# PEER's two tiles of tokens taken one after the other, the first one's listed products in plain float32 beside the second one's routing

## The chip, the cores and the metric

The kernel runs on one core of a Trainium2 chip. The metric is device time in microseconds (us), the median of three runs; lower is better. Engines are named as in the profile: PE multiplies matrices (PEld is its weight load), DVE and ACT work on vectors, POOL issues the indirect transfers, SP issues the ordinary ones.

## The reference, cut to what matters

Two transformer blocks run over 256 tokens of width 1024. Only the last part of the second block is touched by the change, the PEER layer, which picks experts by product keys:

```python
def retrieve(xb):                       # a block of 128 tokens, 8 heads
    q = (xb @ wq).reshape(128, 8, 2, 128)
    s = jnp.einsum('tphq,phkq->tphk', q, keys)            # 2 x 128 scores a head
    top_s, top_i = lax.top_k(s, 16)
    cand = top_s[:, :, 0, :, None] + top_s[:, :, 1, None, :]
    best_s, best_c = lax.top_k(cand.reshape(128, 8, 256), 16)
    i1 = jnp.take_along_axis(top_i[:, :, 0], best_c // 16, axis=-1)
    i2 = jnp.take_along_axis(top_i[:, :, 1], best_c % 16, axis=-1)
    idx = i1 * 128 + i2                                   # one of 16384 experts
    g = jax.nn.softmax(best_s, axis=-1)
    act = gelu(jnp.einsum('tpkd,td->tpk', u_tab[idx], xb))
    return jnp.einsum('tpk,tpkd->td', g * act, v_tab[idx])
```

Every token thus uses 128 (8 x 16) of 16384 experts, each with a row of 1024 numbers in `u_tab` and another in `v_tab`. After it come a residual sum and a last norm.

## The kernel before, in words

The first block and the mixer of the second end at about 702 us of the traced execution; `peer()` is the rest. It never works token by token. It sees the experts as 128 rows (partitions) by 128 columns j, and needs the table A[row, j, token] of weights, which is nonzero for the chosen experts alone. Its steps, for the 256 tokens at once, in two tiles of 128:

- **Heads.** `head(h)` makes the queries of a head for both tiles (16 float32 matmuls 128x256, L1695, each shown in the trace as two passes) and the key scores (4 matmuls, L1708). `topk` (L1490 to L1518) then runs on DVE for both tiles. One `chunk()` per head stands between: 16 float32 matmuls of the same line that make the u products of two columns of all experts ("dense" columns). 19 chunks give D = 38 dense columns in all.
- **Weights and groups.** `weights()` makes softmax weights and transposes the indices. Then 64 groups of 4 tokens: DVE compares an iota with the indices (`o`, L1752) and weights the result (`ow`, L1753), ACT makes `od` (L1754), PE multiplies them (12 float16 matmuls, L1767 and L1769; the latter sums the gates over tokens, the mask of used experts), and the result goes into A (DVE L1773 multiplies it into the dense columns, ACT L1774 copies the rest).
- **Listing.** For the other 90 columns, `listing` packs the experts that occur at all into short lists, in blocks of 4 column pairs (DVE `oq` L1586, ACT `dq` L1588, PE L1597), and writes their row numbers, `rowV` and `rowA`. A goes to tables in DRAM (`keep`).
- **Listed pairs.** A pair is two listed columns of 128 experts. POOL fetches their u and v rows (`uv`, L1879) and their rows of A (`araw`, L1883) by indirect DMA. PE transposes u (L1895), ACT and DVE split it and v into two fp32r parts (L1866, L1867), PE makes u products (`first`, 24 fp32r matmuls 128x256 per tile: three products for one in float32), and then the v products (`second`, 12 fp32r matmuls 128x512 per tile) into the sums `po`. There are 23 pairs with u and v and 10 with v alone (for dense columns). Some serve one tile and some both, 29 and 14 tile passes in all. `uv` has 6 buffers, three pairs' worth.
- **The end.** A branch that handles experts beyond the lists, the residual sum, and the norm.

Each engine works through its own queue in order. A scheduler fixes that order when the program is built: it moves instructions past each other within the queue as far as dependencies and its own time model allow, so program text and queue may differ widely.

## Time and profile before

| | us |
|---|---|
| median of three runs | 1282.18 (1279.02 to 1282.44) |
| the profiled execution's own time | 1270.43 |
| its span in the trace | 1268.4 |
| PE, DVE, ACT, POOL busy in it | 1177.4, 998.0, 664.2, 171.0 |

The span is measured from the first to the last instruction; the profiled execution's own time is 2.03 us longer, and it is 11.75 us below the median of the runs shown. All positions below are us from the start of the span. The busy shares are averages over very different stages, so what follows goes by stage.

### The profile page before, as it was taken

Reading aid. Unit: us, or ns where it says so; the run is one execution under the profiler, and the core shown is the slowest. Engines: PE = TensorE matmul, PEld = TensorE weight load, DVE = VectorE, ACT = ScalarE, POOL = GpSimd, SP = SyncE. Lnnn points to the kernel's source line nnn. Section 1 sums busy time; section 2 is a strip of 40 time slices with the busy share of each in tenths; the row PEclk is TensorE's granted clock in tenths of the full one; section 3 lists DMA queues with packets and bytes.
Section 4 is the critical chain, followed back from the end, with each engine's and each line's share of the span. In section 5 each row is a group of like instructions: output and inputs, shape, how many; then the busy total and the mean of one; then the engine's idle time right before and its main releaser. Section 6 shows DMA issues by size and latency. Waiting matters only on the chain. (4 is left out here: it accounts for less than half of the span.)

```text
span 1268.4 us, 20024 instructions
## 1 busy us (share of the span) xinstructions
PE 1177.4 (93%) x7329; PEld 1024.2 (81%) x7329; DVE 998.0 (79%) x2245; ACT 664.2 (52%) x1118; POOL 171.0 (13%) x169
## 2 busy tenths in 40 slices
PE   8999889999999989999999999989883799999986
PEld 7877667789999878897988888879883688888875
DVE  8999988669988877777887599978887677545766
ACT  6665566644644455657644211146656666444653
POOL 3000000000000000000100000000000756444750
PEclk9999899999999999998999999989996799999998
DMA  6651147647899955554335445422849988556761
GB/s 239 209 170 46 35 157 257 225 133 249 264 307 320 311 194 178 170 161 122 117 92 174 136 150 157 142 91 84 226 141 281 394 326 316 202 175 227 272 224 66
DMA packets 92519, 245.42 MB, mean 193 GB/s; under 512 B 7712, under 2 KB 43200, under 8 KB 85888
## 3 DMA queue, kind: packets, MB, share of 16 engines
q1 hardware_dynamic: 79744, 176.72, 43.8%
q0 software_dynamic: 12672, 67.38, 14.6%
q8 instruction: 59, 0.97, 0.3%
q14 instruction: 44, 0.36, 0.1%
HBM read 224.91 MB, written 19.15 MB: 192 GB/s over the span
## 5 line engine op out<-in xcount | busy, mean ns | idle before, releaser
L209 ACT ACTIVATE whi<-raw 128x1024 fp32r<-128x1024 f32 x176 | 185.4, 1058 | 173.0 <-PE g L216 48.4
L210 DVE TENSOR_TENSOR wlo<-raw,whi 128x1024 fp32r<-128x1024 f32 x176 | 214.7, 1223 | 52.6 <-ACT whi L209 51.6
L1695 PE MATMUL g<-hf,raw 128*128 128x256 f32 x864 | 195.3, 384 | 3.1 <-DVE A L1788 1.6
L1695 PEld LDWEIGHTS g<-hf,raw 128*128 128x128 f32 x864 | 163.2, 192 | 24.7 <-ACT A L1790 2.0
L214 PE MATMUL g<-hfh,whi 128*128 128x256 f32 x352 | 100.7, 287 | 2.6 <-DVE ft L879 2.5
L216 PE MATMUL g<-hfh,wlo 128*128 128x256 f32 x352 | 99.0, 286 | 1.6 <-DVE wlo L210 1.6
L215 PE MATMUL g<-hfl,whi 128*128 128x256 f32 x352 | 100.0, 285 | 0.0
L1879 POOL DMA_INDIRECT uv<-in_uv,rowV x46 | 55.0, 1195 | 323.0 <-DVE rowA L1613 281.3
L1867 DVE TENSOR_TENSOR ul<-ut,uh 128x512 fp32r<-128x512 f32 x92 | 61.9, 687 | 36.8 <-ACT uh L1866 36.4
L1867 DVE TENSOR_TENSOR vl<-uv,vh 128x1024 fp32r<-128x1024 f32 x46 | 56.3, 1226 | 27.2 <-ACT vh L1866 25.2
L1866 ACT ACTIVATE uh<-ut 128x512 fp32r<-128x512 f32 x92 | 52.9, 593 | 45.9 <-PE ut L1895 45.0
L214 PE MATMUL g<-vh,ah 128*128 128x512 f32 x168 | 67.9, 408 | 7.1 <-PEq L1993 3.6
L214 PEld LDWEIGHTS g<-hfh,whi 128*128 128x128 f32 x352 | 67.1, 191 | 3.9 <-DVE ft L879 2.7
L215 PE MATMUL us<-ul,h2h 128*128 128x256 f32 x232 | 68.5, 295 | 0.9 <-DVE ul L1867 0.9
L214 PE MATMUL us<-uh,h2h 128*128 128x256 f32 x232 | 68.7, 296 | 0.2 <-ACT uh L1866 0.2
L216 PEld LDWEIGHTS g<-hfh,wlo 128*128 128x128 f32 x352 | 66.4, 190 | 2.3 <-DVE wlo L210 2.2
L215 PEld LDWEIGHTS g<-hfl,whi 128*128 128x128 f32 x352 | 67.0, 190 | 0.0
L215 PE MATMUL g<-vl,ah 128*128 128x512 f32 x168 | 66.5, 398 | 0.0
L216 PE MATMUL us<-uh,h2l 128*128 128x256 f32 x232 | 65.9, 284 | 0.0
L924 DVE SCALAR_TENSOR_TENSOR wmod<-wmod,cc 128x1024 f32<-128x1024 f32 x48 | 58.7, 1223 | 7.9 <-DMA wmod<-in_w_mod 6.7
L1866 ACT ACTIVATE vh<-uv 128x1024 fp32r<-128x1024 f32 x46 | 48.6, 1058 | 30.0 <-PE g L216 27.6
L216 PE MATMUL g<-vh,al 128*128 128x512 f32 x168 | 63.7, 404 | 0.0
(661 smaller groups left out, 3140.2 us busy)
## 6 DMA issues: line engine op xcount, KB each, us to landing
wmod<-in_w_mod SPq DMA_DIRECT2D x48, 512.0 KB, 5.8
raw<-in_ffn_in SPq DMA_DIRECT2D x44, 512.0 KB, 5.4
raw<-in_pu SPq DMA_DIRECT2D x38, 512.0 KB, 3.7
raw<-in_ffn_out SPq DMA_DIRECT2D x22, 512.0 KB, 4.6
Gd<-A SPq DMA_DIRECT2D x22, 512.0 KB, 6.7
raw<-in_w_out SPq DMA_DIRECT2D x16, 512.0 KB, 3.8
raw<-in_pwq SPq DMA_DIRECT2D x16, 512.0 KB, 3.8
raw<-in_w_qkv SPq DMA_DIRECT2D x12, 512.0 KB, 4.4
```

Source lines behind the costliest of these rows:

```text
L209: self.S.activation(hi, raw, AF.Copy)
L210: self.last_lo = self.V.tensor_sub(lo, raw, hi.bitcast(F32))
L214: a = self.T.matmul(out, ahi, bhi, start=start, stop=False, skip_group_check=True)
L215: self.T.matmul(out, ahi, blo, start=False, stop=False, skip_group_check=True)
L216: b = self.T.matmul(out, alo, bhi, start=False, stop=stop, skip_group_check=True)
L924: i = V.scalar_tensor_tensor(o, w, 1.0, cc[:, j], op0=OP.mult, op1=OP.mult, accum_out=acc)
L1695: T.matmul(p[:, g], w[g][:, k * 128:(k + 1) * 128], hf[:, k], start=k + g == 0, stop=k == 7, skip_group_check=True)
L1866: S.activation(hi, z, AF.Copy)
L1867: V.tensor_sub(lo, z, hi.bitcast(F32))
L1879: P.indirect_dma_start(raw[j], None, vs if k else uv, bass.IndirectOffsetOnAxis(rowV[:, n:n + 1], 0))
```

## The change

Everything in PEER that was done for both tiles together is now done for each tile (`route(tt)`, `listing(..., tt, ...)`, tables and lists per tile), and the two are to overlap: tile 0 is routed and listed first, then its listed pairs run, and `route(1)`, a generator, is stepped between them against a budget of 9 us per pair (8.2 for a top-k of one head, 3.0 for the weights, 1.5 for a group, 1.6 for a listing block). `head(h)` still makes the scores of both tiles; tile 1's are kept in `later` (`sc_7022` in the queues). Dense columns fall from 38 to 14 (7 chunks), so 114 columns are listed, per tile, in 18 u+v pairs and 3 v-only pairs (`caps`), 42 pairs in all. Tile 0's pairs are not split: ACT copies the transposed u, `one` is 8 float32 matmuls 128x256 (L1878) and `two` is 4 float32 matmuls 128x512 (L1908), which read the fetched v itself. Tile 1's pairs keep the three fp32r products. The buffers of `ow` and `od` fall from 3 to 2, those of the dense weights from 5 to 4.

```diff
-        D = 38
-        lims = ((16, 28, 46), (6, 12, 20))
-        NS = 128 - D
+        D = 14
+        caps = (36, 6)
+        NK = (128 - D, D)
...
-            tabs = [dram("Gd", [128 * NS + 128, 256]), dram("Ad", [128 * D + 128, 256])]
+            tabs = [[dram(n + str(tt), [128 * m + 128, 128]) for n, m in zip("GA", NK)] for tt in range(2)]
...
-            rp = rs.enter_context(self.pool("w2", 5))
+            ws0 = ExitStack()
+            rp = ws0.enter_context(self.pool("w2", 4))
...
+            A = [None, None]
+            rt = ExitStack()
+            A[1] = rt.enter_context(self.pool("pa1", side="right")).tile([128, 128, 128], F32, name="A1")
+            qp = rt.enter_context(self.pool("pq", side="right"))
+            op = rt.enter_context(self.pool("oh", AHEAD, side="right"))
+            A[0] = ws0.enter_context(self.pool("pa0")).tile([128, 128, 128], F32, name="A0")
+            later = qp.tile([128, 8, 2, 128], F32, name="sc1")
...
-                s = qp.tile([128, 2, 2, 128], F32, name="sc", bufs=2)
-                S.activation(s, p, AF.Copy)
+                s = qp.tile([128, 2, 128], F32, name="sc", bufs=2)
+                S.activation(s, p[:, 0], AF.Copy)
+                S.activation(later[:, h], p[:, 1], AF.Copy)
...
-            def group(t0, j0):
-                while len(ready) < AHEAD and spread.t < 256:
-                    spread(spread.t)
-                    spread.t += NT
+            def group(t0, tt, j0):
...
+            def keep(tt, want):
                 for k, (lo, hi) in enumerate(((D, 128), (0, min(D, 2 * now["chunk"])))):
...
-            sc = head(0)
...
-            for h in range(8):
-                self.topk(sc, h, qp, idx, best)
+                    while want and now["tokens"][tt] == 128 and kept[k, tt] < hi - lo:
+                        a = kept[k, tt]
+                        b = kept[k, tt] = min(hi - lo, a + 8)
+                        m = NK[k]
+                        i = self.D.dma_start(tabs[tt][k][0:128 * m].rearrange("(p j) t -> p j t", j=m)[:, a:b],
+                                             A[tt][:, lo + a:lo + b])
+                        self.order(self.last_load, i)
+                        want -= 1
...
+            def route(tt, sc):
+                idx = qp.tile([128, 2, 128], F32, name="idx")
+                best = qp.tile([128, 128], F32, name="best")
+                it, wt = (qp.tile([128, 64, 2, 2], F16, name=n) for n in ("idxT", "wgtT"))
+                for h in range(8):
+                    self.topk(sc(h), h, qp, idx, best)
+                    yield 8.2
+                weights(idx, best, it, wt)
+                yield 3.0
+                t0 = 0
+                for g in range(128 // NT):
+                    while len(ready) < AHEAD and t0 < 128:
+                        spread(t0, it, wt)
+                        t0 += NT
+                    group(g * NT, tt, 2 * now["chunk"])
+                    now["tokens"][tt] += NT
+                    yield 1.5
...
+            scs = [head(0)]
+            def first_tile(h):
                 if h < 7:
-                    sc = head(h + 1)
-                chunk()
-            weights()
-            qs.close()
-            with self.pool("oh", AHEAD + 1) as op[0]:
-                for g in range(256 // NT):
-                    if g % 10 == 4:
-                        chunk()
-                    group(g * NT, 2 * now["chunk"])
-                    now["tokens"] += NT
-                    if g % 3 == 2:
-                        keep()
...
-            lister = self.listing(gates, has, f32(it)[:, 0:128], pc, D, lims)
-            rowA, rowV, left = next(lister)
+                    scs.append(head(h + 1))
+                return scs[h]
+            for n, _ in enumerate(route(0, first_tile)):
+                if n in (12, 22, 32):
+                    chunk()
...
+            lister = self.listing(mask, L, has[:, 0], place[:, 0], pc, 0, D, caps)
+            got[0] = next(lister)
             while now["chunk"] < D // 2:
                 chunk()
-                keep(3)
+                keep(0, 4)
                 for _ in range(4):
                     next(lister, None)
-            keep(99)
+            keep(0, 99)
             for _ in lister:
                 pass
...
+            ws0.close()
...
+                    def fetch(s):
+                        o = caps[0] if s.k else 0
+                        ra, rv, _ = got[s.tt]
+                        s.at = vp.tile([128, 2, 128], F32, name="araw", bufs=3)
+                        s.raw = [vp.tile([128, 1024], F32, name="vraw", bufs=2) if s.k else
+                                 vp.tile([128, 2048], F32, name="uv", bufs=6) for _ in range(2)]
+                        for j in range(2):
+                            n = o + 2 * s.c + j
+                            P.indirect_dma_start(s.raw[j], None, vs if s.k else uv,
+                                                 bass.IndirectOffsetOnAxis(rv[:, n:n + 1], 0))
+                        for j in range(2):
+                            n = o + 2 * s.c + j
+                            P.indirect_dma_start(s.at[:, j], None, tabs[s.tt][s.k],
+                                                 bass.IndirectOffsetOnAxis(ra[:, n:n + 1], 0))
+                    def turn(s):
+                        if s.k:
+                            return
+                        s.u = [xp[0].tile([128, 8, 256], F32R, name="u" + n) for n in "hl"] if s.exact else \
+                            [vp.tile([128, 8, 256], F32, name="u")]
+                        for a in range(4):
+                            p = pg.tile([128, 2, 256], F32, name="g").rearrange("p b (j e) -> p b j e", j=2)
+                            for b in range(2):
+                                for j in range(2):
+                                    n = (2 * a + b) * 128
+                                    T.transpose(p[:, b, j], s.raw[j][:, n:n + 128], self.ident)
...
+                            if s.exact:
+                                split(p, *(z[:, n] for z in s.u))
+                            else:
+                                S.activation(s.u[0][:, n], p, AF.Copy)
+                            yield
...
+                        p = self.pst.tile([128, 256], F32, name="t")
+                        for k in range(8):
+                            if s.exact:
+                                self.mm3(p, act.hi[:, k, s.t], act.lo[:, k, s.t], s.u[0][:, k], s.u[1][:, k],
+                                         k == 0, k == 7)
+                            else:
+                                T.matmul(p, hf[:, k, s.t], s.u[0][:, k], start=k == 0, stop=k == 7)
...
+                        v = [z if s.k else z[:, 1024:2048] for z in s.raw]
+                        if s.exact:
+                            s.a = split(a, *(xp[0].tile([128, 2, 128], F32R, name="a" + n) for n in "hl"))
+                            s.v = [split(z, *(xp[0].tile([128, 1024], F32R, name="v" + n, bufs=3) for n in "hl"))
+                                   for z in v]
+                        else:
+                            s.a, s.v = (a,), [(z,) for z in v]
...
+                            if s.exact:
+                                m = self.mm3(po[s.tt][b], *a, *w, start, stop)
+                            else:
+                                m = [T.matmul(po[s.tt][b], a[0], w[0], start=start, stop=stop,
+                                              skip_group_check=True)] * 2
...
+                n0, n1 = caps[0] // 2, caps[1] // 2
+                cols = [(0, c) for c in range(n0)]
+                for c in range(n1):
+                    cols.insert(3 + c * 4, (1, c))
+                NC = len(cols)
+                pairs = [Pair(tt, k, c, tt == 1, n == 0, n == NC - 1) for tt in range(2)
+                         for n, (k, c) in enumerate(cols)]
+                more = route(1, lambda h: later[:, h])
+                budget, fetched, back = 0.0, 0, None
+                act = None
+                NP = len(pairs)
+                for i in range(-1, NP + 1):
+                    if i == NC - 2:
+                        for _ in more:
+                            pass
+                        for _ in lister:
+                            pass
+                        keep(1, 99)
+                        rt.close()
+                        rps.close()
+                        xp.append(ws.enter_context(self.pool("px", 2, side="right")))
+                        for k in range(8):
+                            split(hf[:, k], act.hi[:, k], act.lo[:, k])
+                        x = xp[0].tile([128, 2, 1024], F32, name="x", bufs=1)
+                    while fetched < min(NP if i >= NC - 2 else NC, i + 3):
+                        pairs[fetched].fetch()
+                        fetched += 1
+                    turn = iter(pairs[i + 1].turn() or ()) if i + 1 < NP else iter(())
+                    cur = pairs[i] if 0 <= i < NP else None
+                    if cur:
+                        cur.one()
+                    for _ in range(2):
+                        next(turn, None)
+                    if cur:
+                        cur.weigh()
+                    for _ in turn:
+                        pass
+                    if i < NC - 2:
+                        budget += 9.0
+                        while budget > 0 and more:
+                            t = next(more, None)
+                            if t is None:
+                                more = ()
+                                lister = self.listing(mask, L, has[:, 1], place[:, 1], pc, 1, D, caps)
+                                got[1] = next(lister)
+                                t = 6.0
+                            budget -= t
+                        if not more:
+                            keep(1, 6)
+                            while budget > 0:
+                                next(lister, None)
+                                budget -= 1.6
+                    if i == NP - 3:
+                        left = self.sm.tile([128, 1], F32, name="left")
+                        n = self.nc.values_load(ln[0:1, 0:1], min_val=0, max_val=32768,
+                        with self.tc.If(n > 0):
+                            rest()
+                        self.D.dma_start(x.rearrange("p t d -> p (t d)"), xd)
+                        norm(0)
+                    if back:
+                        back.two()
+                    back = cur
+                norm(1)
```

`topk`, `weights`, `chunk` and `listing` are cut to one tile in the same manner, with half the elements in each instruction that handled both.

What this makes of the queues can be read from the built programs. First DVE, in the groups of tile 0 (A is the table, `t` the product of a group in PSUM). Before:

```order
L1753 TENSOR_TENSOR ow<-o,wgtT 128x1024
L1752 TENSOR_TENSOR o<-iof,idxT 128x1024
L1773 TENSOR_TENSOR A<-A,t 128x16x4
L1753 TENSOR_TENSOR ow<-o,wgtT 128x1024
L1773 TENSOR_TENSOR A<-A,t 128x16x4
```

And now, at the same place (`A_7021` is tile 0's table, `tks`, `tky`, `tkz`, `tki`, `tkf` are top-k's tiles, and `sc_7022` holds the scores of tile 1):

```order
L1489 MATCH_REPLACE tky<-tks,sc_7022 128x128
L1758 TENSOR_TENSOR A_7021<-A_7021,g 128x2x56
L1724 TENSOR_TENSOR o<-iof,idxT 128x1024
L1725 TENSOR_TENSOR ow<-o,wgtT 128x1024
L1513 TENSOR_TENSOR tkz<-tkz,tkf 128x512
L1490 MAX tks<-tky 128x8
L1743 TENSOR_TENSOR A_7021<-A_7021,t 128x4x4 x2
L1725 TENSOR_TENSOR ow<-o,wgtT 128x1024
L1724 TENSOR_TENSOR o<-iof,idxT 128x1024
L1514 TENSOR_REDUCE idx<-tkz 128x2x16
L1493 CAST tkf<-tki 128x32
```

Tile 1's top-k, which the program text puts beside tile 0's pairs, stands in DVE's queue between tile 0's groups. Counted along the queue, the heads of tile 1 end after groups 6, 10, 18, 20, 28 and 30 of tile 0's 32, and the last two within the first two listing blocks of tile 0; none is left beside tile 0's pairs.

Next PE, in a pair of tile 0 after all routing (`g<-ident,uv` are transposes of u, `t<-u,hf` is `one`, `t<-ident,us` the transposes in `weigh`, `po<-uv,ua` is `two`):

```order
L1908 MATMUL po<-uv,ua 128x512 x4
L1878 MATMUL t<-u,hf 128x256 x2
L1859 MATMUL g<-ident,uv 128x128 x8
L1888 MATMUL t<-ident,us 128x128 x2
L1878 MATMUL t<-u,hf 128x256 x2
L1859 MATMUL g<-ident,uv 128x128 x4
L1878 MATMUL t<-u,hf 128x256 x4
L1859 MATMUL g<-ident,uv 128x128 x4
```

The four `po` matmuls are the last readers of a pair's `uv` buffers, and the same buffers are transposed from again three pairs on. The transposes of the next pair start one `t<-u,hf` block after each `po` block.

Last PE again, where tile 1's indices are transposed (L1705) beside the first pairs of tile 0, after seven of them, and its groups begin (`od`, `ow`):

```order
L1888 MATMUL t<-ident,us 128x128 x2
L1705 MATMUL t<-ident,idx 128x128 x2
L1705 MATMUL t<-ident,best 128x128
L1859 MATMUL g<-ident,uv 128x128 x4
L1908 MATMUL po<-uv,ua 128x512 x4
L1908 MATMUL po<-vraw,araw 128x512 x4
L1859 MATMUL g<-ident,uv 128x128 x5
L1736 LDWEIGHTS od
```

In the queue there follow nine groups of tile 1 with nothing but 23 transposes among them, then a pair for every six groups or so, and the last six groups again without a product of a pair.

## Rows read from the trace of the kernel before

**Rows 1.** The page's part 1, PE.

```profile
PE 1177.4 (93%) x7329; PEld 1024.2 (81%) x7329; DVE 998.0 (79%) x2245; ACT 664.2 (52%) x1118; POOL 171.0 (13%) x169
```

**Rows 2.** Busy us by stretch: PE, PEld, DVE, ACT, POOL; PEclk, DMA, GB/s.

```profile
714.70:831.10 116.40, 110.89 (x541) 98.13 (x539) 114.37 (x495) 17.30 (x27) 0.00 (x0) 0.99 0.50 150
836.00:941.50 105.50, 100.61 (x984) 91.20 (x983) 87.76 (x190) 66.55 (x135) 0.00 (x0) 1.00 0.49 142
941.50:956.70 15.20, 11.25 (x90) 9.76 (x89) 10.27 (x29) 3.92 (x8) 0.00 (x0) 1.00 0.72 198
956.70:990.30 33.60, 10.98 (x130) 9.68 (x131) 22.84 (x71) 26.20 (x36) 7.23 (x8) 0.54 1.01 294
1000.00:1220.00 220.00, 216.37 (x1397) 192.67 (x1397) 138.14 (x191) 120.82 (x191) 127.67 (x114) 1.00 0.74 266
```

**Rows 3.** PE in order of time, heads: start us, us, instruction.

```profile
719.02 1.05 PE L1708 MATMUL t<-keys,pq 128*128 128x128 f32 x8
719.92 11.82 PE L1695 MATMUL g<-hf,raw 128*128 128x256 f32 x54
731.57 1.06 PE L1708 MATMUL t<-keys,pq 128*128 128x128 f32 x8
```

**Rows 4.** The waits in the groups, 836 to 941.5: total, times, longest.

```profile
DVE A L1773 <- PE t L1767: 15.6, 13, 3.4
```

**Rows 5.** Groups of instructions by line, PEER alone: busy us, mean ns.

```profile
L1752 DVE TENSOR_TENSOR o<-iof,idxT 128x1024 f16<-128x1024 f16 x64 | 43.6, 689 | 2.1 <-ACT od L1754 0.8
L1753 DVE TENSOR_TENSOR ow<-o,wgtT 128x1024 f16<-128x1024 f16 x64 | 43.6, 688 | 0.0
L1773 DVE TENSOR_TENSOR A<-A,t 128x72 f32<-128x72 f32 (+6 forms) x64 | 15.0, 246 | 16.6 <-PE t L1767 16.6
```

**Rows 6.** DVE in order of time, the first comparison of the groups.

```profile
833.06 1.28 DVE L1752 TENSOR_TENSOR o<-iof,idxT 128x1024 f16<-128x1024 f16 x2
```

**Rows 7.** PE in order of time, float16 matmuls of the groups.

```profile
912.16 0.62 PE L1767 MATMUL t<-ow,od 128*128 128x128 f16 x8
912.62 0.39 PE L1769 MATMUL gates<-ow,od 128*128 128x128 f16 x4
```

**Rows 8.** DVE in order of time, two listing blocks.

```profile
956.75 0.69 DVE L1586 TENSOR_TENSOR oq<-iof,pq 128x1024 f16<-128x1024 f16 x1
958.62 0.69 DVE L1586 TENSOR_TENSOR oq<-iof,pq 128x1024 f16<-128x1024 f16 x1 [0.54 <-ACT dq L1588]
```

**Rows 9.** All engines in order of time, from list to first pair.

```profile
980.94 1.12 POOL L1879 DMA_INDIRECT uv<-in_uv,rowV  x1 [281.29 <-DVE rowA L1613]
983.79 0.95 POOL L1883 DMA_INDIRECT araw<-Gd,rowA  x1 [0.31 <-issue]
983.86 0.69 DVE L1586 TENSOR_TENSOR oq<-iof,pq 128x1024 f16<-128x1024 f16 x1 [0.68 <-ACT dq L1588]
990.30 1.08 PE L1895 MATMUL ut<-ident,uv 128*128 128x128 f32 x3
```

**Rows 10.** PE in order of time, the listed pairs.

```profile
1061.42 0.39 PE L216 MATMUL g<-vh,al 128*128 128x512 f32 x1
1061.64 0.28 PE L215 MATMUL us<-ul,h2h 128*128 128x256 f32 x1
1061.76 0.28 PE L216 MATMUL us<-uh,h2l 128*128 128x256 f32 x1
1062.24 1.04 PE L1895 MATMUL ut<-ident,uv 128*128 128x128 f32 x8
1063.03 0.48 PE L214 MATMUL g<-vh,ah 128*128 128x512 f32 x1
```

**Rows 11.** Indirect transfers of 990 to 1230: issues, median us to landing.

```profile
uv<-in_uv,rowV POOLq DMA_INDIRECT x42, 7.7
```

**Rows 12.** PE's wait at the branch; then the chain's first step after PE.

```profile
1235.59 0.77 PE L214 MATMUL g<-vh,ah 128*128 128x512 f32 x1 [3.60 <-PEq L1993]
1258.02 0.70 DVE gy L2008
```

More of the change, by code (lines that the diff above doesn't have):

```diff
@@ L1521, in listing @@
-    def listing(self, gates, has, place, pc, D, lims):
+        tf, c2 = (tp.tile([128, 2, 16], F16, name=n) for n in ("tkf", "tkc2"))
+        z = tp.tile([128, 256], F32, name="tkz")
+        t = tp.tile([128, 2, 16], F32, name="tks")
+        ti = tp.tile([128, 2, 16], U32, name="tki")
+        for p in range(2):
+            x = sc[:, p]
+            y = tp.tile([128, 128], F32, name="tky")
+            V.max(t[:, p, 0:8], x)
+            V.match_replace(y, t[:, p, 0:8], x, -3e38)
+            V.max(t[:, p, 8:16], y)
+            V.max_index(ti[:, p, 0:8], t[:, p, 0:8], x)
+            V.max_index(ti[:, p, 8:16], t[:, p, 8:16], y)
@@ L1576, in listing @@
-            cp = ls.enter_context(self.pool("blk", side="right"))
+            new, before, rk = (cp.tile([128, 128], F32, name=n) for n in ("new", "before", "rk"))
+            P.memset(new, 1.0)
+            P.memset(new[:, 0:1], 0.0)
+            P.memset(new[:, D:D + 1], 0.0)
+            V.tensor_scalar(before, self.jp, 0.0, None, op0=OP.is_gt)
+            V.tensor_scalar(has, mask, 0.0, None, op0=OP.is_gt)
+            V.tensor_tensor_scan(rk, new, has, 0.0, op0=OP.mult, op1=OP.add)
+            p = self.pst.tile([128, 2], F32, name="t")
@@ new lines, in listing @@
+            for n, r in enumerate(keys):
+                T.matmul(p[:, n:n + 1], before, rk[:, r.stop - 1:r.stop], start=n == 0, stop=True,
+                         skip_group_check=True)
+            base = self.sm.tile([128, 2], F32, name="base")
+            V.tensor_copy(base, p)
+            for n, r in enumerate(keys):
+                V.scalar_tensor_tensor(place[:, r], rk[:, r], base[:, n:n + 1], has[:, r], op0=OP.add, op1=OP.mult)
+            V.tensor_scalar(place, place, -1.0, None, op0=OP.add)
@@ L1847, in peer @@
[L1847 to L1857 removed]
+            halves = slice(0, 512), slice(512, 1024)
@@ new lines, in two @@
+                            a, w = [z[:, j] for z in s.a], [z[:, halves[b]] for z in s.v[j]]
+                            start, stop = s.first and j == 0, s.last and j == 1
+                            if s.exact:
[3 more added lines that the diff above has]
+                                              skip_group_check=True)] * 2
```

450 lines of the change are left out of this document (152 added, 298 removed).

## Prediction

> **What bounds the kernel now.** I read the busy shares first, then the same by stretch of PEER, then the waits, and only then single instructions. PE is busy 93% of the span [rows 1], but PEER's stretches have different bounds [rows 2]. While the heads are scored (714.7 to 831.1) DVE is busy for 114.4 of 116.4 us: 16 top-k passes (8 heads, two tiles) at 7.15 us each, with PE's dense chunks beside them. In the groups (836 to 941.5) PE is busy for 100.6 of 105.5, DVE for 87.8, and DVE's largest wait is 15.6 us for a group's product [rows 4]. From 941.5 to 990.3 PE is busy for only 22.2 of 48.8 us: lists are made, and the first pair is awaited. In 1000 to 1220, the listed pairs, PE is busy for 216.4 of 220. So there are 27 us of idle PE between groups and pairs to win, and 10.4 after PE's last product, from 1258.0 to the end at 1268.4 [rows 12].
>
> **PE's prices.** After a keys block, 54 float32 passes 128x256 run from 719.92 to 731.57 [rows 3]: 0.216 us each, 0.43 for a matmul of two, 6.9 for 16. A keys block takes 0.90. In the pairs an fp32r matmul 128x256 starts 0.12 after the one before, one of 128x512 takes 0.22 to 0.23, and 8 transposes 0.79, 0.099 each [rows 10]. A group's 12 float16 matmuls take 0.69, since 8 take 0.46 [rows 7].
>
> A check of them on the old loop: 23 pairs x 16 transposes (36), 29 x 24 first products (84), 29 x 0.25 for weighing (7) and 504 second products (116) make 243 us. The loop took 1258.0 - 990.3 = 267.7 [rows 9, 12], of which some 8.5 at the branch (PE's wait there is 3.6 [rows 12]; by my estimate the reload of x holds as much again, and the rest is slower clock), so about 16 us, 7%, were lost otherwise.
>
> **The change: PE's work.** 12 fewer chunks save 12 x 6.9 = 83 us. A u+v pair of tile 0 costs 16 x 0.099 + 8 x 0.43 + 0.25 + 4 float32 matmuls 128x512. No float32 matmul of that width stands in these rows. As low bound I take three fp32r products (0.69), as high bound two passes each as long as a whole fp32r row (2 x 0.48 = 0.96 [rows 10]); I use 0.86, twice the 256-wide one, which is the same two passes. That is 8.7 us; a v-only pair is 3.4. 18 and 3 of them make 167. A pair of tile 1 costs 1.58 + 24 x 0.12 + 0.25 + 12 x 0.23 = 7.5, a v-only one 2.8: 143 in all. Together 310 against 243 before, 67 more. So on PE alone the change saves 83 - 67 = 16 us; with the 27 above, 43 is the most it can win, if nothing new stands idle. The rest of the forecast is what stands idle.
>
> **Heads.** Top-k now runs for one tile while the heads are scored, so PE sets the pace: 16 x 0.43 + 0.90 = 7.8 per head. Seven heads after the first score at 714.7 end at 769.3, and the last top-k 7.15 later, at 776.5 instead of 831.1: 54.6 gained. The first comparison followed 2 us behind that [rows 6], so it now starts at 778.5.
>
> **Tile 0's groups.** Here the order decides. Tile 1's eight top-k passes stand in DVE's queue within these groups and just behind, about 6.45 of them before the last group. DVE has 32 x 1.38 (`o` and `ow` [rows 5]) = 44, 32 small multiplications at about 0.1 = 3 (0.25 before, on up to 38 columns, now 2 to 6), 6.45 x 7.15 = 46 of top-k, and 1 for chunks and weights: 94 us. PE has 32 x 0.69 and 48 dense matmuls in that time, 43 us, so DVE sets the end: 778.5 + 94 = 873, against 941.5. Without tile 1's top-k it would be 827. That work is not new, but it was to lie beside tile 0's pairs, where DVE has little else to do, and now it stands ahead of everything that waits for tile 0's list.
>
> **Tile 0's list.** A block takes 958.62 - 956.75 = 1.87 [rows 8], the single `oq` buffer going from DVE to ACT and back; 15 blocks instead of 12 stand before the first fetch: 28. The prologue took 15.2 [rows 2]; with one class instead of three and no chunk in it I take 9 (bounds 5 and 15). 1.55 top-k heads are left, 11 us, of which gaps between blocks take perhaps 6: 5 more. So the first fetch goes out at 873 + 42 = 915, and the first transposes follow 9.4 later, as before (980.94 to 990.30 [rows 9]): 925. That is 65 us earlier than before.
>
> **Tile 0's pairs.** 167 of pairs, 22 for tile 1's 32 groups on PE, 10 for its list (PE's 11.0 in 956.7 to 990.3 bounds it [rows 2]) and 1 of transposes: 200 at PE's pace. On top:
> - 8 for the start: the granted clock was 0.54 in the stretch ahead of the pairs, close to the 1.2 GHz level, where PE was busy for 11 of 33.6 us [rows 2]; it will be so again, and I take it that 8 us of the first work cost twice their time.
> - 10 for fetches. A pair's `uv` buffers are free only after its `two`, and are transposed from three pairs later; by the queue, 8.7 + 0.86 = 9.6 us of PE work lie between. A fetch takes 1.1 to issue and 7.7 to land [rows 9, 11], the second column 1.3 more: 10.1. So about 0.5 us late in each of 18 pairs. Before, v was split into copies, which freed the buffer earlier.
> - 17 for tile 1's groups. The first nine and the last six have no products of pairs among them, and go at DVE's pace, 1.55 against 0.69: 13. The `ow` buffers are two now, so bursts of four groups wait too: 4.
> - 8 for tile 1's listing, 17 blocks of which some wait at 1.87 with little else in the queue; 4 for the 8.4 MB of tile 1's table, written beside the fetches (29 us of full DMA at 294 GB/s [rows 2], mostly in idle share); 2 at the boundary of the tiles.
> These 49 (24% of 200) are the softest part: 7% as in the old loop would be 14, and fetches 3 us late would be 45 more.
>
> Taking away tile 0's splits saves nothing: in 1000 to 1220 DVE and ACT were busy for 138 and 121 of 220 [rows 2], so PE covered them.
>
> **Tile 1's pairs and the end.** 143, plus 5 for fetches and 8 for branch and reload of x: 156. Then 10.4.
>
> **Sum.** 925 + 200 + 49 + 156 + 10.4 = 1340.4 against a span of 1268.4: 72 longer. The profiled execution of before took 1270.4 and the median is 1282.2; adding 72 to the median gives **1354**.
>
> **A rule against the trace.** Fetch issues by POOL now run beside DVE's comparisons for half of the pairs. One row shows it: an `araw` issue at 983.79 took 0.95 while a comparison ran from 983.86 for 0.69 [rows 9], no longer than issues elsewhere. The Trainium skill, "SBUF — State Buffer", section "Who interferes with whom", says that GpSimd and some VectorE instructions (two-port modes, or two SBUF inputs against a GpSimd read) exclude each other on a shared port pair, one blocking until the other has finished. By that rule issues would be held in those pairs; by the row they are not. I go by the row, and price the other as a rival.
>
> **Rivals.**
> 1. *Tile 1's top-k hides in waits of tile 0's groups.* For it: DVE did wait 15.6 us in 64 groups. Against it: that is 8 in 32, and there are 46 to hide, in a stretch where PE has only 43 us of work. If it hid wholly, everything comes 46 earlier: 1308. Chance 7%.
> 2. *Faster.* The mechanism is overlap at PE's own pace: PE never waits for tile 1's routing or for fetches, so the loops lose 7% as before (24 instead of the 54 above, 30 less). By itself that gives 1324, within my forecast's own range. To end faster it needs the list of tile 0 early too: it decides at first transposes before about 883 (925 - 42), which means the groups done by 831, where I have 873. With rival 1 in full and this one: 1354 - 46 - 30 = 1278, and with the low bound for the float32 products (84 x 0.17 = 14) 1264. Chance 6%, and 3% for a result inside 0.3%.
> 3. *Fetches set the pace.* If transfers land 3 us later than the median says, because tile 1's table is written beside them and tile 0's raw buffers are held to the end, each of 18 pairs loses 3 more: 1354 + 54 = 1408. Chance 7%.
> 4. *POOL's issues are held by DVE.* If each of a pair's 4 issues waits for one comparison (0.69), that is 2.8 per pair in nine pairs with groups or blocks beside them: 25, so 1379. Chance 4%.
>
> **Chances and range.** The forecast, late list and some stalls, has 73%: by itself 1320 to 1380. A measurement here can tell about 0.3% (the three runs lie that close). The 8-in-10 range leaves out rivals 2 (in full) and 3 and reaches to rival 1 below; above it takes in rival 4 and the high bound of float32 products (84 x 0.10 = 8): 1308 to 1390. Faster 6%, same 3%, slower 91%.
>
> **What would show it.** Right: first `o` near 778; `MAX`, `MATCH_REPLACE` on `sc` among tile 0's groups with DVE all but full; first `uv` issue near 915, transposes near 925; tile 0's last `two` near 1174 with PE idle in its loop for some 40 us, put down to DVE's `ow` and `A` and to `uv` transfers; `one` 3.4 us and `two` 3.4 us a pair; the end near 1340. Wrong: a list before 890 (DVE is faster at top-k between groups than alone, or the prologue is shorter), a loop whose PE idle is under 20 us (the fetches come in time), or a `uv` wait in nearly every pair (rival 3). What I trust least is the 49 us of stalls, since no stretch of before mixes routing with pairs.

## The result

| | before | after |
|---|---|---|
| median of four runs, us | 1280.74 (1279.02 to 1282.44) | 1321.19 (1318.36 to 1325.07) |
| profiled execution's own time | 1270.43 | 1318.36 |
| its span | 1268.4 | 1316.6 |

The change made the kernel slower by 3.2%: the ratio of its runs to those of before is 1.0318, 95% interval [1.0286, 1.0350]. The forecast was 1354, in a range of 1308 to 1390. The profiled execution of before was 10.3 us quicker than the median of its runs, that of after 2.8, so the spans lie 48.2 apart where the medians lie 40.5 apart.

Positions count from the start of the span, and the executions do not reach PEER at the same time, though the program ahead of it was not changed. PE's first query matmul of PEER, before, after and in hold_topk below:

```profile
696.53 1.46 PE L1695 MATMUL g<-hf,raw 128*128 128x256 f32 x6
```

```profile
690.20 1.46 PE L1673 MATMUL g<-hf,raw 128*128 128x256 f32 x6
```

```profile
697.10 1.46 PE L1677 MATMUL g<-hf,raw 128*128 128x256 f32 x6
```

So where two kernels are compared below, times are counted from this matmul. By it PEER took 571.9 us before and 626.4 after, 54.5 more; the spans differ by less because the execution of after came to PEER 6.3 us earlier.

PE's busy time hardly moved (1177.4 in [rows 1]); what grew is the span. The page's first part, of after:

```profile
span 1316.6 us, 19977 instructions
PE 1184.4 (90%) x7235; PEld 993.7 (75%) x7235; DVE 962.7 (73%) x2277; ACT 688.1 (52%) x1172; POOL 201.6 (15%) x211
```

The stretches of after, cut at the steps that the prediction named (columns as in [rows 2]): heads, tile 0's groups, its list, the wait for the first fetch, four pieces of tile 0's pairs (pairs alone; with tile 1's groups; with its list; pairs alone), and tile 1's pairs.

```profile
714.00:776.50 62.50, 54.36 (x274) 47.82 (x272) 60.37 (x262) 11.98 (x24) 0.00 (x0) 0.95 0.42 136
776.50:860.10 83.60, 55.15 (x480) 47.95 (x480) 83.60 (x297) 39.67 (x72) 0.00 (x0) 0.83 0.12 39
860.10:900.80 40.70, 24.76 (x190) 21.39 (x190) 31.69 (x107) 28.13 (x44) 0.03 (x1) 0.71 0.52 207
900.80:907.00 6.20, 0.32 (x7) 0.36 (x7) 1.41 (x9) 1.00 (x2) 4.86 (x5) 0.50 0.68 239
907.00:980.00 73.00, 70.14 (x353) 49.44 (x354) 10.99 (x26) 23.57 (x44) 40.09 (x47) 0.96 0.83 298
980.00:1044.70 64.70, 55.81 (x475) 43.80 (x475) 37.55 (x84) 36.48 (x73) 14.86 (x14) 0.95 0.32 112
1044.70:1094.40 49.70, 45.37 (x296) 33.18 (x294) 24.78 (x76) 32.57 (x54) 16.91 (x16) 0.93 0.86 332
1094.40:1143.40 49.00, 45.27 (x207) 31.60 (x206) 10.98 (x25) 17.98 (x35) 20.68 (x22) 0.97 0.70 246
1143.40:1306.20 162.80, 149.67 (x984) 132.17 (x983) 110.78 (x165) 92.78 (x151) 80.87 (x72) 0.98 0.70 245
```

To be seen: in tile 0's groups DVE is busy for 83.60 of 83.60 us and PE for 55. In the pairs, PE is busy for 216.6 of 236.4 us (tile 0) and 149.7 of 162.8 (tile 1). DVE is nearly empty in the first 73 us of the pairs, 11 us busy: this is where the program text had put tile 1's top-k.

DVE in order of time, near the end of tile 0's groups:

```profile
854.33 0.69 DVE L1724 TENSOR_TENSOR o<-iof,idxT 128x1024 f16<-128x1024 f16 x1
854.93 0.29 DVE L1490 MAX8 tks<-tky 128x8 f32<-128x128 f32 x1
855.14 0.68 DVE L1724 TENSOR_TENSOR o<-iof,idxT 128x1024 f16<-128x1024 f16 x1
855.73 1.06 DVE L1514 TENSOR_REDUCE idx<-tkz 128x32 f32<-128x512 f16 x1
...
856.79 0.17 DVE L1743 TENSOR_TENSOR A<-A,t 128x24 f32<-128x24 f32 x1
856.88 0.69 DVE L1725 TENSOR_TENSOR ow<-o,wgtT 128x1024 f16<-128x1024 f16 x1
857.48 0.17 DVE L1743 TENSOR_TENSOR A<-A,t 128x24 f32<-128x24 f32 x1
857.57 0.69 DVE L1725 TENSOR_TENSOR ow<-o,wgtT 128x1024 f16<-128x1024 f16 x1
...
858.25 0.41 DVE L1501 MATCH_REPLACE8 tkz<-best,tkc 128x256 f32<-128x256 f32 x1
858.64 0.28 DVE L1491 FIND_INDEX8 tki<-tks,sc 128x8 uint32<-128x128 f32 x1
```

`MAX8`, `TENSOR_REDUCE`, `MATCH_REPLACE8`, `FIND_INDEX8` are tile 1's top-k, in between the groups' `o`, `ow` and A, with no idle time anywhere. The `ow` at 856.88 is shown with 0.69 us, but the next instruction starts 0.60 later: a price taken from durations alone is too high by a seventh.

The chain from list to first pair, POOL and then PE:

```profile
900.77 1.13 POOL L1841 DMA_INDIRECT uv<-in_uv,rowV  x1 [208.61 <-DVE rowA L1592]
```

```profile
906.99 0.66 PE L1859 MATMUL g<-ident,uv 128*128 128x128 f32 x2 [4.83 <-DMA uv<-in_uv,rowV]
909.71 2.70 PE L1859 MATMUL g<-ident,uv 128*128 128x128 f32 x10 [2.06 <-DMA uv<-in_uv,rowV]
...
1110.23 3.60 PE L1908 MATMUL po<-uv,ua 128*128 128x512 f32 x8
1113.67 0.59 PE L1878 MATMUL t<-u,hf 128*128 128x256 f32 x2
```

The first fetch goes out at 900.77 and the first transposes start at 906.99. Further down a pair of tile 0 as PE does it: eight passes of `po` in 3.44 us, 0.86 for a float32 matmul 128x512, as priced.

What PE's loop waited for in tile 0's pairs (engine, line, waited for: total, times, longest):

```profile
PE g L1859 <- DMA uv<-in_uv,rowV: 12.7, 5, 4.8
PEld g L1859 <- DMA uv<-in_uv,rowV: 9.0, 5, 2.6
DVE A L1743 <- PE t L1736: 8.5, 4, 2.7
POOL uv L1841 <- PE po L1908: 25.8, 24, 3.5
```

### The profile page after: what moved, and what is told of

It reads as the page before. It is cut to its first block, busy times and chain, and to the rows that moved or that the text cites. A ratio compares the mean times of both kernels' runs of the same rounds, so it can differ in the third digit from the quotient of the medians.

```text
span 1316.6 us, 19977 instructions
## 1 busy us (share of the span) xinstructions
PE 1184.4 (90%) x7235; PEld 993.7 (75%) x7235; DVE 962.7 (73%) x2277; ACT 688.1 (52%) x1172; POOL 201.6 (15%) x211
## 5 line engine op out<-in xcount | busy, mean ns | idle before, releaser
L1673 PE MATMUL g<-hf,raw 128*128 128x256 f32 x480 | 112.0, 391 | 3.2 <-ACT A L1760 3.2
L1673 PEld LDWEIGHTS g<-hf,raw 128*128 128x128 f32 x480 | 92.4, 196 | 16.3 <-ACT A L1760 3.9
L1859 PE MATMUL g<-ident,uv 128*128 128x128 f32 x576 | 88.2, 283 | 15.9 <-DMA uv<-in_uv,rowV 12.7
L1859 PEld LDWEIGHTS g<-ident,uv 128*128 128x128 f32 x576 | 69.3, 145 | 29.7 <-issue 11.5
L1845 POOL DMA_INDIRECT araw<-G,rowA x72 | 73.5, 1021 | 97.4 <-DVE ua L1890 37.6
L1736 PE MATMUL t<-ow,od 128*128 128x128 f16 x512 | 53.9, 234 | 29.3 <-DVE ow L1725 18.0
L1824 DVE TENSOR_TENSOR ul<-g,uh 128x512 fp32r<-128x512 f32 x72 | 48.4, 687 | 38.8 <-ACT uh L1823 34.0
L1878 PE MATMUL t<-u,hf 128*128 128x256 f32 x288 | 75.5, 403 | 0.0
L1736 PEld LDWEIGHTS <-od 128*128 128x128 f16 x512 | 43.3, 103 | 35.0 <-issue 20.3
L1908 PE MATMUL po<-uv,ua 128*128 128x512 f32 x144 | 65.5, 594 | 0.2 <-DVE ua L1890 0.2
```

Of the source, the lines that this page charges most:

```text
L1673: T.matmul(p[:, g], w[g][:, k * 128:(k + 1) * 128], hf[:, k], start=k + g == 0, stop=k == 7, skip_group_check=True)
L1736: T.matmul(p[:, k], d[:, k], w[:, k // 2, i, :, k % 2], start=k + i == 0, stop=i == 1, skip_group_check=True)
L1845: P.indirect_dma_start(s.at[:, j], None, tabs[s.tt][s.k], bass.IndirectOffsetOnAxis(ra[:, n:n + 1], 0))
L1859: T.transpose(p[:, b, j], s.raw[j][:, n:n + 128], self.ident)
L1878: T.matmul(p, hf[:, k, s.t], s.u[0][:, k], start=k == 0, stop=k == 7)
L1908: m = [T.matmul(po[s.tt][b], a[0], w[0], start=start, stop=stop, skip_group_check=True)] * 2
```

## The experiments

All ratios are to the kernel before, run on the same chip; its median there is given. The steps in the profiles, in us from PEER's first query matmul:

| | first comparison | first fetch | end |
|---|---|---|---|
| before | 136.5 | 284.4 | 571.9 |
| after | 86.3 | 210.6 | 626.4 |
| hold_topk | 82.7 | 177.0 | 593.7 |
| dense10 | 87.1 | 210.4 | 621.4 |
| hold_dense10 | 84.3 | 174.1 | 585.2 |
| woven3 | 86.1 | 170.6 | 580.7 |
| woven2 | 92.5 | 171.4 | 582.0 |
| woven2_even | 95.7 | 176.8 | 595.7 |
| woven2_late | 82.7 | 160.3 | 567.9 |

**hold_topk.** Nothing but the place of tile 1's top-k is changed: its first instructions may not stand ahead of the one that ends tile 0's list of u+v pairs.

```diff
-            V.max(t[:, p, 0:8], x)
+            m = V.max(t[:, p, 0:8], x)
+            if after:                      # tile 1: self.listed, the write of rowA of tile 0
+                self.order(after, m)
```

> The changed kernel, with the top-k of tile 1 held on DVE until the list of tile 0 is written (eight passes, 57 us of DVE, now beside tile 0's first pairs). Theory: DVE was busy for 85.5 of the 85.5 us of tile 0's groups, so about 46 us of top-k stood on the path; the groups then end some 36 us earlier (PE has 46 us of work there), the first transposes come at about 871 instead of 907, the pairs take up to 8 us longer because DVE now has both, and the time falls by 28 to 40, to 1281 to 1293. Rival: the top-k filled waits that come back as waits for PE or ACT, and the time falls by less than 8. Second rival, the port rule: POOL's fetch issues beside top-k take longer than 0.95 us and the first pairs lose 10 us or more, so the time falls by about 20.

Measured: 1292.32 (before 1280.45), ratio 1.0081 [1.0061, 1.0102]; 29 us below the change as it was made. The stretches of it (groups, list, wait for the fetch, tile 0's pairs):

```profile
779.80:836.50 56.70, 47.54 (x480) 42.79 (x480) 42.73 (x98) 36.24 (x72) 0.00 (x0) 0.94 0.16 54
836.50:874.00 37.50, 22.40 (x190) 19.32 (x190) 24.03 (x74) 25.26 (x39) 0.00 (x0) 0.79 0.58 230
874.00:880.20 6.20, 0.31 (x7) 0.27 (x7) 6.17 (x42) 1.06 (x2) 4.87 (x5) 0.50 0.66 231
880.20:1115.40 235.20, 212.02 (x1319) 153.27 (x1320) 135.11 (x439) 113.14 (x206) 94.85 (x98) 0.97 0.67 245
```

The groups took 56.7 us instead of 83.6, and the first fetch left 177.0 us behind PEER's first query matmul instead of 210.6. Of these 33.6 us, 3.6 lie ahead of the first comparison, 26.9 in the groups and 3.2 in the list. Tile 0's pairs took 235.2 against 236.4 although DVE now did eight top-k passes beside them: it is busy for 135 us there. So the top-k had cost some 30 us on the path (33.6 in these two executions, 29 by the medians), and beside the pairs it costs nothing that shows. The size was at the lower end of what was expected (the groups end 30 us earlier, not 36), because without top-k the groups are paced by PE and DVE waiting on each other, neither full. Both rivals fall: the time did not come back as other waits, and though some of POOL's issues were held (last section), the pairs lost nothing.

**plain_both.** Tile 1's pairs in plain float32 too.

```diff
-                pairs = [Pair(tt, k, c, tt == 1, n == 0, n == NC - 1) ...
+                pairs = [Pair(tt, k, c, False, n == 0, n == NC - 1) ...
```

> The changed kernel, with tile 1's pairs in plain float32 like tile 0's, without splits (output a little different in its last digits). Theory: the pairs run at PE's price, which is 1.2 us higher for a u+v pair (18) and 0.6 for a v-only pair (3) in float32: the time rises by 18 to 24, to about 1342. Rival: tile 1's pairs wait for splits or for fetches, not for PE: the time stays within 8 of 1321, or falls.

Measured: 1342.47 (before 1280.45), ratio 1.0471 [1.0430, 1.0512]; 21 us more than with the splits. The price difference of PE alone is 23. So tile 1's pairs run at PE's price, and the splits, which take ACT's and DVE's time, cost them nothing that shows.

**dense10.** Two chunks and one v-only pair per tile fewer, with lists long enough as they are (the input of dense weights is cut to five chunks with it).

```diff
-        D = 14
-        caps = (36, 6)
+        D = 10
+        caps = (36, 4)
```

> The changed kernel with 10 dense columns instead of 14: two chunks fewer (13.8 us of PE) and one v-only pair fewer in each tile (3.4 and 2.8 us of PE); the list lengths still fit. Theory: the two chunks stood beside tile 0's listing, where PE was busy for 18 of 33 us, so they cost next to nothing there, and only the v-only pairs count: 5 to 10 less, 1311 to 1316. Rival: all PE work is on the path: 20 less, 1301.

Measured: 1314.76 (before 1280.45), ratio 1.0249 [1.0217, 1.0282]; 6.4 less. The first fetch, in this kernel's POOL row, did not move forward:

```profile
901.88 1.13 POOL L1841 DMA_INDIRECT uv<-in_uv,rowV  x1 [208.35 <-DVE rowA L1592]
```

901.88 against 900.77, or 210.4 against 210.6 from PEER's first query matmul: the 13.8 us of dense matmuls taken out beside the list gained nothing there. The 6.2 us of v-only pairs were gained, as far as runs can tell whose intervals are 0.3% to either side: the two loops took 392.2 instead of 399.2. Here PE's work counted where PE was the last to be ready, and not beside the list.

**hold_dense10.** Both edits.

> Both edits together, top-k held and 10 dense columns. Theory: the two gains add, 33 to 50 less than 1321: 1271 to 1288, at or below the kernel before (1281). Rival: with the list earlier, the two chunks' place is filled otherwise and the second edit gives nothing: as hold_topk.

Measured: 1281.06 (before 1280.45), ratio 0.9991 [0.9970, 1.0011]: 40 us below the change, level with before. The gains add: 29 and 6 alone, and 40 together, which agrees within the noise.

**woven3, woven4.** What was left in hold_dense10 was a list with PE idle (busy for 10.7 of 33.1 us) and groups with dense matmuls in their way. The edit ties each held dense matmul to a listing block.

```diff
-                if n in (12, 22, 32):
+                if n in (4, 10):
                     chunk()
...
+            ms = [next(lister) for _ in range(15)]
+            ms = [m for m in ms for _ in range(3)]
             while now["chunk"] < D // 2:
-                chunk()
-                keep(0, 4)
-                for _ in range(4):
-                    next(lister, None)
+                chunk(ms)                  # the n-th held matmul behind block n // 3
```

With it all writes of tile 0's table (`keep`) now stand behind the held chunks in the program.

> hold_dense10 with its five chunks placed otherwise: two go ahead of tile 0's groups, none among them, and three are woven between tile 0's listing blocks, three dense matmuls behind each of 15 blocks. In hold_dense10 the groups took 56.7 us with PE busy for 47.2 and DVE for 42.7, waiting on each other, and the list after them 33.1 with PE busy for 10.7. Theory: PE's idle time stands in the list and its work in the groups; with the dense work moved, DVE paces the groups (43 to 48 us, 9 to 13 less), and the list takes 0 to 4 us longer, so first fetch and end come 6 to 12 earlier: 1269 to 1275, faster than the kernel before (1280.5). Rival: the groups are paced by their two buffers, not by dense work beside them, and the list grows by what they win: within 4 of 1281.

> The same with one chunk ahead of the groups and four behind the listing blocks, four dense matmuls behind each (1.72 us, and about 0.6 of listing on PE, against a block period of 1.81 to 1.87). Theory: PE now paces the list at 2.3 us a block instead of 1.85, 7 us longer in all, and the heads win nothing since DVE paces them: 5 to 8 above woven3. Rival: block and dense work overlap freely, as woven3.

Measured, on one chip where the kernel before took 1272.77: woven3 1275.47, ratio 1.0024 [1.0008, 1.0040]; woven4 1279.10, 1.0062 [1.0039, 1.0085]. woven4 against woven3 came out as expected in sign and a little small in size (3.6). woven3 missed: it is not faster than before. The groups took 44.7 us, the list with the dense work in it 33.3, and the list was written at 854.5, counted from PEER's first query matmul 10 us earlier than in hold_dense10 (15 by position). But then, in its POOL row, the first PE rows of its pairs, and SP's issues ahead of them:

```profile
861.04 1.13 POOL L1846 DMA_INDIRECT uv<-in_uv,rowV  x1 [6.01 <-DMA G<-A]
```

```profile
866.91 0.66 PE L1864 MATMUL g<-ident,uv 128*128 128x128 f32 x2 [10.96 <-DMA uv<-in_uv,rowV]
870.09 2.71 PE L1864 MATMUL g<-ident,uv 128*128 128x128 f32 x10 [2.52 <-DMA uv<-in_uv,rowV]
```

```profile
833.76 4.82 SPq L1673 DMA_DIRECT2D raw<-in_pu  x2
838.62 17.57 SPq L1775 DMA_DIRECT2D G<-A  x15
```

The first fetch waited until 861.04 for the writes of tile 0's table: its buffers take the place of A, and the writes stood in SP's queue behind weights of the held chunks (L1673), for which there were not enough buffers. The rows themselves then came no later than elsewhere: the transposes start 5.9 us behind the fetch (6.2 in after), and the second wait is 2.52 (2.06 in after). The waits of 13.5 that the next expectation puts down to the writes are thus the 6 us above and an ordinary landing. Of the 10 us that the list gained, 6 went to a transfer, not to the engines; what the profile keeps, 4.5 us of PEER against hold_dense10, the medians do not show (1.0024 against 0.9991).

**woven2, woven2_even.** Two held chunks, whose weights fit the four buffers; the other three at `n in (2, 5, 9)` and, for woven2_even, `(1, 3, 5)` with two matmuls per block.

> woven3 with three chunks ahead of tile 0's groups and two behind the listing blocks (three dense matmuls a block). In woven3 the list of tile 0 was written at 854.5 against 869.5 in hold_dense10, but the first fetch waited 6 us for the writes of tile 0's table (they stood in the queue behind the weights of the held chunks, which waited for buffers), and the first pairs 13.5 more for their rows beside these writes. With two held chunks their weights fit the four buffers and no write waits. Theory: the table is written under the listing again, the fetch goes out right behind the list at about 856, transposes at 862 and without the waits; 8 to 14 us below woven3, 0.4 to 1.0% below the kernel before. Rival: the waits behind the list are those of the fetch itself, beside other transfers: within 3 us of woven3.

> As woven2, with the three early chunks further ahead, among the heads, and two dense matmuls behind each listing block instead of three. Theory: the heads are paced by DVE's top-k (7.15 us a head, PE 7.8 with its keys), so chunks there push the last top-k back by some of their 20 us of PE work: 3 to 10 above woven2. Rival: PE has room among the heads, and the two are within 2 us.

Measured, with before at 1282.59: woven2 1280.14, 0.9982 [0.9963, 1.0001]; woven2_even 1289.84, 1.0060 [1.0035, 1.0085]. woven2 missed too: it is 0.4% below woven3 by the ratios, not 8 to 14 us, and level with before. The wait behind the list was gone, as expected, but the early chunks held back the heads: PE was full until 776, and the first comparison came 92.5 us behind PEER's first query matmul, 8 later than in hold_dense10 (84.3) and 6 later than in the change. With chunks still further ahead, in woven2_even, it came at 95.7, and the time was worse by 9.7, as expected (3 to 10). The stretches of woven2: heads, from there to the first comparison, and groups:

```profile
714.00:776.00 62.00, 62.00 (x312) 55.23 (x311) 53.05 (x214) 10.13 (x23) 0.00 (x0) 1.00 0.46 150
776.00:788.60 12.60, 5.09 (x27) 3.95 (x25) 9.05 (x40) 2.41 (x5) 0.00 (x0) 0.76 0.28 83
788.60:833.20 44.60, 29.55 (x384) 27.08 (x384) 42.33 (x100) 36.03 (x66) 0.00 (x0) 0.88 0.01 1
```

**woven2_late.** The same, the three chunks at `n in (6, 14, 22)`, which puts their 37 matmuls behind the last keys.

> woven2 with the three early chunks emitted later, so that their 37 matmuls stand behind the last keys, around the transposes of the indices, ahead of tile 0's first group, and none among the heads. In woven2 PE was busy for 62.0 of 62 us in the heads and the first comparison came at 788.6 instead of 776.5 to 779.8, which ate what the groups (44.6 us instead of 56.7) had won. Theory: PE has some 10 us of room there while the last top-k runs on DVE; the first comparison comes near 780, the groups end near 827 and the first fetch goes out near 861, 6 us earlier than in woven2: 4 to 8 us less than it, 0.5 to 0.9% below the kernel before. Rival: the 37 matmuls (16 us) hold the first group's products back by as much, and nothing is won over woven2.

Measured, with before at 1279.14: 1264.35, ratio 0.9888 [0.9851, 0.9925], so 1.1% faster than before. Against woven2, by the ratios, it is 0.9% or some 12 us less, more than the 4 to 8 expected. Its stretches (heads, groups, list, wait, tile 0's pairs, tile 1's):

```profile
714.00:776.90 62.90, 62.90 (x321) 55.85 (x320) 59.87 (x246) 13.20 (x27) 0.00 (x0) 1.00 0.42 149
776.90:820.20 43.30, 28.07 (x394) 24.94 (x392) 42.31 (x102) 35.07 (x68) 0.00 (x0) 1.00 0.06 19
820.20:854.50 34.30, 23.54 (x194) 18.76 (x194) 23.60 (x76) 25.77 (x39) 0.00 (x0) 0.86 0.62 246
854.50:860.40 5.90, 0.23 (x3) 0.17 (x3) 5.90 (x39) 0.04 (x1) 4.67 (x5) 0.50 0.68 239
860.40:1091.70 231.30, 211.18 (x1314) 153.47 (x1315) 133.98 (x438) 113.03 (x206) 90.99 (x95) 0.96 0.66 244
1091.70:1251.40 159.70, 147.66 (x973) 129.91 (x972) 107.93 (x162) 90.80 (x148) 76.55 (x68) 0.98 0.69 242
```

The groups end at 820.2 and the first fetch leaves at 854.5; counted from PEER's first query matmul that is 50 us earlier than in the change and 11 earlier than in woven2, 10 of them in the heads. The 37 matmuls cost nothing there: the first comparison comes at 82.7, as in hold_topk, which has none of them. PE has no idle time in the heads (62.9 of 62.9), and the groups are paced by DVE (42.3 of 43.3); only the list still goes at the pace of the exchange between DVE and ACT. The pairs are what they were but for the v-only pair, 231.3 and 159.7.

## Why the prediction was right, and where it was off

The sign, the place and the mechanism held. Step by step, predicted and then measured in the profile of after:

| step | predicted | measured |
|---|---|---|
| first comparison | 778.5 | 776.5 |
| tile 0's groups, from there | 94, to 873 | 83.6, to 860.1 |
| list to the first fetch | 42, to 915 | 40.7, to 900.8 |
| fetch to the first transposes | 9.4, to 925 | 6.2, to 907.0 |
| tile 0's pairs | 249, to 1174 | 236.4, to 1143.4 |
| tile 1's pairs | 156, to 1330 | 162.8, to 1306.2 |
| the end | 10.4 | 10.4 |

The agreement of the first line is in part luck. The forecast took the arrival at PEER from the profile of before; counted from PEER's first query matmul it put the first comparison at 82.0 us and it came at 86.3, which the 6.3 us of earlier arrival hid. Without tile 1's top-k, in hold_topk, it came at 82.7: the heads were priced rightly, and the top-k costs time there already.

**Tile 1's top-k in tile 0's groups** was the step that decided, and hold_topk shows it: 29 us of the 40.5 lost. The term was mis-sized in two ways. The durations of `o` and `ow` (0.69) were taken as their pace, which is 0.60: 64 x 0.09 = 5.8 too much. And some 18 instructions of tile 1's first two heads, about 5 us by their durations, stand in DVE's queue ahead of the first `o`, in the heads (DVE busy for 60.4 of 62.5 us), where they cost 3.6. The price of leaving it there is also not its 46 us of work but some 30, as said above, since other waits take its place; rival 1 as written ("hides wholly") was too crude at both ends.

**The pairs at PE's price** held. The float32 matmul 128x512 took 0.86, the value used between 0.69 and 0.96; plain_both moved by 21 where the prices say 23. Over both tiles the pairs and what runs beside them were put at 405 us and took 399.2; tile 1's alone took 6.8 more than put down, with PE busy for 149.7 against a price of 143.

**The stalls** (49) were the softest part and too high: 236.4 - 200 = 36. PE's busy time was 216.6, some 17 above the price; by an estimate from the granted clock of 0.95 over the stretch, some 11 of them are the clock. PE's idle time is 19.8, not the 40 forecast, and just under the 20 that the prediction named as a sign of being wrong. Of it, waits for `uv` rows are 7.9 on PE, in four waits of 1.2 to 2.4 (the 12.7 above takes in the 4.8 ahead of the first pair). So the term for fetches (10) was near in sum but not in kind: not half a microsecond in each of 18 pairs, but four waits, three of them among tile 1's groups, and most fetches in time. The pieces with tile 1's groups and list lose 8.9 and 4.3, against 17 and 8 put down. That the sum still came near is in part chance, since slower clock made up for waits that did not come.

**The fetch** was taken at its old 9.4 us and took 6.2. In the old kernel other transfers ran beside it (DMA's share was 0.95 from 980.94 to 990.30); here DMA had been idle for 10 us (share 0.00). In the other changed kernels it took 5.9 to 6.1, but 8.2 in woven4, where writes of tile 0's table still ran beside it. That points to the other transfers; no run changes them alone.

**The reference point.** The sum was made against the profiled execution, and its 72 us were added to a median that lay 12 us above it. The two profiled executions did not lie equally far from their medians, which accounts for 8 of the 33 us by which the forecast was too high; 24 are in the table, 6.3 of them the earlier arrival at PEER and not any step of the kernel, and the median of before moved by 1.4.

**The rule on the shared port** was set aside on the strength of one row, and that row was misread. It showed an issue that had begun 0.07 us *before* the comparison. In after, eight of 33 issues between 975 and 1095 took 1.33 to 1.43 us; each began 0.08 to 0.18 us after an `ow` or `oq` had begun, as here (DVE, then POOL, in order of time):

```profile
1054.76 0.69 DVE L1565 TENSOR_TENSOR oq<-iof,pq 128x1024 f16<-128x1024 f16 x1 [0.29 <-ACT dq L1567]
```

```profile
1054.86 1.41 POOL L1845 DMA_INDIRECT araw<-G,rowA  x1 [0.30 <-issue]
```

Three more issues, which began 0.48 to 0.49 us into an `o`, took 1.02 or 1.03. So an issue is held for what is left of the instruction. The Trainium skill, "SBUF — State Buffer", section "Who interferes with whom", says that a VectorE instruction with two SBUF inputs contends with a GpSimd instruction that reads SBUF. The trace agrees where DVE came first; where the issue came first, neither was held: the row of the prediction shows 0.95 and 0.69. In all it cost about 0.45 us for each of the eight issues, and 3.8 of POOL's time in that stretch with the three others, against 25 in rival 4, because only an issue that begins while such an instruction runs is caught. Other rows of before had shown it too: 38 of its 132 issues began behind a `vl<-uv,vh` or `vl<-vraw,vh` (1.23 us) and took up to 1.99 (last section).

**Why the change loses, in all.** Counted from PEER's first query matmul, the pairs start 77.0 us earlier than before (216.8 against 293.8; by position 907.0 and 990.3 [rows 9]), and from there to the last product the two loops take 399.2 instead of 267.7. Of these 131 more, 67 are pairs that serve one tile where an old one could serve two (by the prices, of which plain_both checks the difference between the two kinds), 32 are tile 1's routing and listing on PE (by the prices too), and 32 are what is left, waits and slower clock, 57 against 25. What should have been overlapped and was not, the top-k, is most of the loss, 29 of 40.5, but not all: with it held the kernel is still 0.8% slower than before. With that order, fewer dense columns and the rest put where PE idles it is faster than both kernels, by 1.1% against the one before.

## What to carry to other kernels

Work is beside other work only if the queue says so: read what a scheduler made of the program, and price what the moved instructions now stand in front of. One ordering edge was worth 29 us here, more than any other single edit. Take work out where its engine is the last to be ready (dense10: 13.8 us of matmuls for nothing in one place, 6.2 for 6.4 in another), and when a stage is made shorter, look at once for the transfer that was hidden behind it (woven3). And compare two traces from the start of the stage, not of the span: here the same work ahead of PEER ended up to 7 us apart.

## What the runs showed of the hardware that was not expected

An indirect fetch issued by POOL is held by an instruction of DVE with two operands in SBUF that began before it, for what is left of that instruction; with one of the operands in PSUM it is not. An issue alone takes 0.94 to 0.95 us. In before, one that began 0.14 us into the second of these two `vl` (both operands in SBUF) took 1.90:

```profile
1085.49 2.58 DVE L1867 TENSOR_TENSOR vl<-uv,vh 128x1024 fp32r<-128x1024 f32 x2 [6.08 <-ACT vh L1866]
```

```profile
1086.99 1.90 POOL L1879 DMA_INDIRECT uv<-in_uv,rowV  x1 [4.63 <-DVE vl L1867]
```

One that began 0.35 us into a `ul`, whose `ut` is in PSUM, took 0.94:

```profile
1077.30 0.69 DVE L1867 TENSOR_TENSOR ul<-ut,uh 128x512 fp32r<-128x512 f32 x1
```

```profile
1077.65 0.94 POOL L1883 DMA_INDIRECT araw<-Ad,rowA  x1 [3.09 <-DVE al L1867]
```

In all of before, 38 issues that began 0.05 to 1.1 us into a `vl` of 1.23 took 0.96 to 1.99, the longer the earlier they began, and 27 that began 0.05 to 0.55 us into a `ul` of 0.69 took 0.93 to 0.95. In after the comparisons and `ow` do the same: 1.33 to 1.43 for issues that began 0.08 to 0.18 us into 0.69, 1.02 or 1.03 for those at 0.48 to 0.49. The issue that began 0.07 ahead of a comparison was not held, nor the comparison (0.69) behind it [rows 9]. Beside top-k, in hold_topk, issues that began 0.01, 0.14, 0.18 and 0.36 us into a float16 multiplication 128x512 (0.68) took 1.50, 1.36, 1.32 and 1.15, while issues that began beside `MAX8`, `FIND_INDEX8` or `TENSOR_REDUCE` alone took 0.93 to 0.95, but for the first fetch of all (1.12, as in every kernel here).
